# Both parts of v in one operand for both directions of an mLSTM, with the second sum in the bank of the scores

## The chip, the cores and the metric

The kernel runs on one core of a Trainium2 chip. Its engines are TensorE (PE in the profile, with PEld for the loads of its weights), VectorE (DVE), ScalarE (ACT), GpSimd (POOL) and SyncE (SP), whose queue issues most of the transfers. The time is what the device takes for one launch, in microseconds (us). Before the change three runs took 2744.58, 2746.43 and 2747.94 us; the median is 2746.43.

## The reference

One encoder layer is applied to two sequences, of 1024 and 2048 tokens, each with 16 meta tokens in front. One projection of the normalised input feeds two branches, a windowed attention over a grid and a bidirectional mLSTM; both are gated, projected, merged and put out through a last projection. What matters here is the chunkwise mLSTM, which runs once forwards and once on the flipped sequence:

```python
def _encoder_layer(h, ...):
    xn = _rmsnorm(h, g_pre)
    proj = xn @ w_in + b_in
    ya = (_neighbourhood_attention(...) * silu(na_z)) @ w_a
    yb = (_mlstm_branch(...) * silu(ml_z)) @ w_b
    y = (ga * ya + gb * yb) @ w_out
    return h + _rmsnorm(y, g_post)

def _mlstm_chunkwise(q, k, v, ig, lf):
    ...
    S = einsum('bhnjd,bhnsd->bhnjs', q, k) * exp(logD - m_t[..., None])
    e_inter = exp(inter - m_t)
    num = einsum('bhnjs,bhnsv->bhnjv', S, v) + e_inter[..., None] * einsum('bhnvk,bhnjk->bhnjv', Cs, q)
    den = sum(S, -1) + e_inter * einsum('bhnk,bhnjk->bhnj', ns, q)
    return num / maximum(abs(den), exp(-m_t))[..., None]
```

All data are 32-bit floats.

## The kernel before

**Products of split numbers.** Every 32-bit operand of a product is split into a high part, rounded to the format that TensorE multiplies at full pace, and a low part, the rest. `mm3` (L165) adds three products: high by high, high by low, low by high. The last one, low by low, is dropped.

**Two programs woven into one.** TensorE runs in the order in which the program is written; the order on the other engines is set by a scheduler that knows the dependences. `run` walks through two generators. `dense` yields after every few products of the projections (L170 to L172 with 512 columns, L607 to L609 with 256, L1592 to L1594) and says what they cost; `sparse` goes through the four steps mLSTM of the short sequence, attention of the short one, mLSTM of the long one, attention of the long one. Each time that `sparse` yields a cost, so much of `dense` is written before `sparse` goes on. One yield in the mLSTM has the cost 1.82 (`A_A`): between two of its steps stand 6 or 12 products of 512 columns, or as many columns in products of 256.

**The mLSTM.** The 96 chunks of 128 tokens (four heads, 8 chunks of the short and 16 of the long sequence) are taken two at a time, as 48 blocks. `ml_states` makes the states of a head; `ml_outputs` then goes through its blocks b with p = b - 1 behind it. In one turn of its loop are six yields. `scores(b)` makes the products of k and q (L1344, L1345) in the one bank `sc` of PSUM and copies a part with ScalarE (L1347); `scores_up(b)` adds the other part on VectorE (L1352) and multiplies by the decays of the two directions (L1357, L1358); `scores_lo(b)` makes the low parts (L1364). `back(p, j)` is the output of chunk j of the block before: the state's part with three products of 260 columns into a bank `tr` (L170 to L172), scaled by ScalarE into `num` (L1377, twice), and the part with v into a bank `sm`, added to `num` by VectorE (L1383, L1384). For direction 0 of that part the operand is `v2`, where the high part of v (130 columns: 128, a column of ones for `den`, and one of zeros) and the low part lie side by side, so that one product of 258 columns (L1380) and one of 130 (L1381) do for three; direction 1 takes `mm3` with three products of 130 columns. One bank has 512 columns; the two directions use 388. `decay`, `conv_*`, `load`, `kv` and `state` prepare the next block; `finish(p)` divides.

PSUM has eight banks: three `pj` for the projections, two `tr`, one `sc`, two `sm`. A bank is handed on only when its last reader is through.

**x, and where it is kept.** `build_half` makes the operand x of 512 tokens of the long sequence: rows of the mean squares by a product with ones (`rrows`, L329, copied by ScalarE at L330), then eight scalings on VectorE (L477), four roundings on ScalarE (L484) and four subtractions on VectorE (L485). For the short sequence it is L343 and L344. A half that is needed again later is stored in memory in 16 pieces of 256 KB, put in the queue `xput` by `xkeep`; `beside`, which is called after every yield of `dense`, issues one of them in every second call (L503), and `xparts` issues what is left before the next half is built (L334).

**The attention's start.** `na` loads for its first head q, k, v and the gate (`na_prep`, L847 to L862), then the position bias (`na_bias`, L835), all through the queue of SP.

Of the kernel before, what the change touches and what calls it, by code (L numbers as in the profile page):

```python
# [13 lines left out]
ALU = mybir.AluOpType  # L14
# [3 lines left out]
P = 128  # L18
# [41 lines left out]
def _row_types(R):  # L60

    out = []
    for t in range(R // 8):
        if t == 0:
            out.append((0, 0, 11))
        elif t == R // 8 - 1:
            out.append((2, R - 12, 12))
        else:
            out.append((1, 8 * t - 4, 15))
    return out  # L70
# [48 lines left out]
A_NA, A_D, A_A, A_G = 1.085, 1.63, 1.82, 1.3  # L119


class K:
# [376 lines left out]
    def beside(self):  # L499

        self.turn += 1
        if self.xput and self.turn % 2:
            self.nc.sync.dma_start(*self.xput.popleft())  # L503


# [262 lines left out]
    def na(self, s, rts):  # L768

        tc, nc, i = self.tc, self.nc, self.i  # L770
        rows = _row_types(SEQLEN[s] // 64)
        with tc.tile_pool(name=f"na{s}{rts[0]}", bufs=1, side="right", reuse_waits="tile") as np_:
            self.qB = [np_.tile([P, 4, P], F32R, name=f"qB{j}") for j in range(2)]
            self.kx = [np_.tile([P, 16, 64], F32R, name=f"kx{j}") for j in range(2)]
            self.gts = [np_.tile([P, 17, 48], F32, name=f"gt{j}") for j in range(2)]
            for q in self.qB:
                nc.gpsimd.dma_start(q[64:128], i["onehot"].rearrange("a (b c) -> a b c", b=4))
            for g in self.gts:
                nc.gpsimd.memset(g[:, 0, :], 0.0)
                nc.gpsimd.memset(g[:, 16, :], 0.0)  # L780
            heads = [(rt, pr, hh) for rt in rts for pr in range(4) for hh in range(2)]
            n = len(heads)
            prep = self.na_prep(np_, s, rows, heads, 0)
            for k in range(6):
                next(prep, None)
                for _ in range(2 if k else 17 - 11 * s):
                    yield A_NA
            self.na_bias(rows, heads, 0)
            cur, nxt = self.head, None
            units = [(j, cb) for j in range(n) for cb in range(4)]  # L790
            ready = {}
            n_ = len(units)
            for u in range(n_ + 4):
                if u >= 4:
                    self.na_copy(ready[u - 4])
                if u < n_:
                    j, cb = units[u]
                    if cb == 0:
                        cur = self.head
                        prep = self.na_prep(np_, s, rows, heads, j + 1) if j + 1 < n else iter(())  # L800
                        next(prep, None)
                    ready[u] = [cur, heads[j], cb, None, None, self.gts[j % 2], None]
                    self.na_scores(np_, ready[u], rows)
                    if j + 1 < n and cb == 0:
                        self.na_bias(rows, heads, j + 1)
                yield A_NA
                if u < n_:
                    self.na_exp(np_, ready[u])
                if 1 <= u <= n_:
                    self.na_scale(np_, ready[u - 1])  # L810
                if u >= 4:
                    self.na_add(ready.pop(u - 4), s)
                if u < n_ and cb:
                    next(prep, None)
                if u == n_ + 3:
                    break
                yield A_NA
                if 2 <= u <= n_ + 1:
                    self.na_turn(np_, ready[u - 2])
                    if u < n_ and cb >= 2:  # L820
                        next(prep, None)
                yield A_NA
                if 2 <= u <= n_ + 1:
                    self.na_low(ready[u - 2])
                if u >= 3:
                    self.na_out(ready[u - 3])
                yield A_NA
# [426 lines left out]
    def ml_outputs(self, mp, s, h, g, NB, sts, norms):  # L1254

        nc = self.nc
# [18 lines left out]
        def gates(b):  # L1275

            if b % 2:
                tzs[b // 2] = [mp.tile([P, 4, P], F32, name=n, tag="tz", bufs=2) for n in ("tog", "szg")]
                for x, d in zip(tzs[b // 2], (self.TO, self.SZ)):
                    nc.sync.dma_start(x, d[s][(b - 1) * BL:(b + 1) * BL, h * P:(h + 1) * P].rearrange("(c p) f -> p c f", p=P))  # L1280

        def conv_a(b):
            if b < NB:
                convs[b] = self.conv(mp, raws.pop(b), h, False, BL)
                next(convs[b])
# [15 lines left out]
        def kv(b):  # L1301
            if b < NB:
                kf = kfs.pop(b)
                kh = mp.tile([P, CB, P], F32R, name="kh", tag="kh", bufs=2)
                kl = mp.tile([P, CB, P], F32R, name="kl", tag="kl", bufs=2)
                nc.scalar.activation(f2(kh), kf, AF.Copy)
                nc.vector.tensor_tensor(f2(kl), kf, f2(kh).bitcast(F32), op=ALU.subtract)
                kss[b] = kh, kl
# [30 lines left out]
        def scores(b):  # L1339

            (kh, kl), (qh, _, q2) = kss.pop(b), qs[b]
            s0 = self.psum("sc", [P, CB, 2, P])
            for j in range(CB):
                nc.tensor.matmul(s0[:, j], kh[:, j], q2[:, j], start=True, stop=False)  # L1344
                nc.tensor.matmul(s0[:, j, 0], kl[:, j], qh[:, j], start=False, stop=True)  # L1345
            s1 = mp.tile([P, CB, P], F32, name="s1", bufs=1)
            nc.scalar.activation(s1, s0[:, :, 1], AF.Copy)  # L1347
            shs[b] = s0, s1

        def scores_up(b):  # L1350
            s0, s1 = shs[b]
            nc.vector.tensor_tensor(s1, s0[:, :, 0], s1, op=ALU.add)  # L1352
            sh = mp.tile([P, 2, CB, P], F32R, name="sh", tag="bh", bufs=2)
            sl = mp.tile([P, 2, CB, P], F32R, name="sl", tag="bl", bufs=2)
            for d in range(2):
                um = ums[b][d]
                nc.vector.tensor_tensor(um, um, s1, op=ALU.mult)  # L1357
                nc.scalar.activation(f2(sh[:, d]), f2(um), AF.Copy)  # L1358
            shs[b] = sh, sl
# [6 lines left out]
        def back(b, j):  # L1366
            sh, sl = shs[b]
            (vh, vl, v2), (qh, ql, _) = vs[b], qs[b]
            cch, ccl = cs[b]
            cc = 1 + b * CB + j  # L1370
            pi = self.psum("tr", [P, 512])
            self.mm3(pi[:, :260], qh[:, j, :], ql[:, j, :], cch[:, j], ccl[:, j])
            if j == 0:
                nums[b] = mp.tile([P, CB, 2, 130], F32, name="num", bufs=1)
            num = nums[b]
            for d in range(2):
                nc.scalar.activation(num[:, j, 1 - d], pi[:, 130 * d:130 * d + 130], AF.Copy, scale=g[d]["e"][:, cc, h:h + 1])  # L1377
            pa = self.psum("sm", [P, 512])
            self.mm3(pa[:, 0:130], sh[:, 1, j, :], sl[:, 1, j, :], vh[:, j, :], vl[:, j, :])
            nc.tensor.matmul(pa[:, 130:388], sh[:, 0, j, :], v2[:, j, 0:258], start=True, stop=False)  # L1380
            nc.tensor.matmul(pa[:, 130:260], sl[:, 0, j, :], vh[:, j, :], start=False, stop=True)  # L1381
            nj = num[:, j].rearrange("p d c -> p (d c)")
            nc.vector.tensor_tensor(nj, pa[:, :260], nj, op=ALU.add)  # L1383
            nc.vector.tensor_tensor(num[:, j, 1, 0:P], pa[:, 260:388], num[:, j, 1, 0:P], op=ALU.add)  # L1384

        def finish(b):
            num = nums.pop(b)
# [32 lines left out]
        for b in range(NB + 1):  # L1420
            p = b - 1
            if p >= 0:
                gates(p)
            if b < NB:
                scores(b)
                conv_a(b + 1)
            yield A_A
            if p >= 0:
                back(p, 0)
            if b < NB:  # L1430
                scores_up(b)
            yield A_A
            if b < NB:
                scores_lo(b)
            conv_b(b + 1)
            load(b + 2)
            decay(b + 1, 0)
            yield A_A
            if p >= 0:
                back(p, 1)  # L1440
            decay(b + 1, 1)
            conv_c(b + 1)
            yield A_A
            kv(b + 1)
            if p >= 0:
                finish(p)
            yield A_A
            state(b)
            yield A_A

# [361 lines left out]
```

## Time and profile before

| | |
|---|---|
| median of three runs | 2746.43 us |
| the profiled execution | 2745.8 us |
| its span in the trace | 2744.0 us |
| granted TensorE clock, mean | 0.999 |
| share of the span: PE, PEld, DVE, ACT, POOL | 99%, 89%, 66%, 49%, 1% |
| transfers | 661.08 MB, mean 241 GB/s |
| chain of waits that ended last, shares of the span | PE 94%, DMA 4%, DVE 1% |

Work before the first instruction and behind the last of the span takes 1.8 us (2745.8 - 2744.0). A row of a group gives line, engine, operation, tile written <- tiles read, shape, count | busy time in us, mean ns of one | idle time of the engine just before them and what ended it. A row of the order of time gives the start in us from the span's start, the duration, and then the same, with the idle time in brackets. Starts of a product and of its weights' load overlap with what runs before them, so the pace of TensorE is read from the distances of starts and not from durations.

### The profile page before, as it was taken

Reading aid. Unit: us, or ns where it says so; the run is one execution under the profiler, and the core shown is the slowest. Engines: PE = TensorE matmul, PEld = TensorE weight load, DVE = VectorE, ACT = ScalarE, POOL = GpSimd, SP = SyncE. Lnnn points to the kernel's source line nnn. Section 1 sums busy time; section 2 is a strip of 40 time slices with the busy share of each in tenths; the row PEclk is TensorE's granted clock in tenths of the full one; section 3 lists DMA queues with packets and bytes.
Section 4 is the critical chain, followed back from the end, with each engine's and each line's share of the span. In section 5 each row is a group of like instructions: output and inputs, shape, how many; then the busy total and the mean of one; then the engine's idle time right before and its main releaser. Section 6 shows DMA issues by size and latency. Waiting matters only on the chain.

```text
span 2744.0 us, 48160 instructions
## 1 busy us (share of the span) xinstructions
PE 2724.6 (99%) x16888; PEld 2429.5 (89%) x16888; DVE 1801.9 (66%) x5082; ACT 1343.7 (49%) x3236; POOL 16.1 (1%) x104
## 2 busy tenths in 40 slices
PE   9999999999999999999999999999999999999998
PEld 8998898999789988988988888888888989989898
DVE  5332688766556755467768667575668788897854
ACT  5122556445444454255566655564555655556421
POOL 0000000000000000000000000000000000000000
PEclk9999999999999999999999999999999999999999
DMA  9655768855875644686866689577559798999965
GB/s 368 201 183 196 254 212 318 273 165 199 312 222 159 193 143 135 179 314 218 275 233 233 234 293 307 180 240 233 181 192 308 231 337 255 319 293 281 322 238 204
DMA packets 375203, 661.08 MB, mean 241 GB/s; under 512 B 46800, under 2 KB 195744, under 8 KB 374960
## 3 DMA queue, kind: packets, MB, share of 16 engines
q1 hardware_dynamic: 373840, 655.31, 71.7%
q0 software_dynamic: 1120, 2.69, 0.5%
q8 instruction: 133, 2.18, 0.3%
q14 instruction: 110, 0.90, 0.1%
HBM read 455.64 MB, written 202.22 MB: 240 GB/s over the span
## 4 chain that ended last, share of the span: by engine, by line
PE 94%; DMA 4%; DVE 1%; ACT 0%; issue 0%; SPq 0%; DVEq 0%; ACTq 0%
PE pj L170 17%; PE pj L171 17%; PE pj L172 17%; PE pj L607 7%; PE pj L608 7%; PE pj L609 7%; PE pj L1592 3%; PE pj L1594 3%; PE pj L1593 3%; PE sm L946 3%; PE tr L931 3%; DMA wraw<-wu 1%; PE sm L172 1%; PE sm L171 1%; PE sm L170 1%; PE sc L899 1%
## 5 line engine op out<-in xcount | busy, mean ns | idle before, releaser
L170 PE MATMUL pj<-xh,whi 128*128 128x512 f32 (+1 forms) x1792 | 704.7, 393 | 0.7 <-ACT whi L264 0.6
L171 PE MATMUL pj<-xl,whi 128*128 128x512 f32 (+1 forms) x1792 | 688.7, 384 | 0.1
L172 PE MATMUL pj<-xh,wlo 128*128 128x512 f32 (+1 forms) x1792 | 687.9, 384 | 0.3 <-DVE wlo L265 0.3
L607 PE MATMUL pj<-whi,xh 128*128 128x256 f32 (+1 forms) x1536 | 439.6, 286 | 1.6 <-DMA whi<-wh 1.6
L608 PE MATMUL pj<-wlo,xh 128*128 128x256 f32 (+1 forms) x1536 | 433.2, 282 | 1.9 <-DMA wlo<-wl 1.9
L609 PE MATMUL pj<-whi,xl 128*128 128x256 f32 (+1 forms) x1536 | 433.0, 282 | 0.0
L172 PEld LDWEIGHTS pj<-xh,wlo 128*128 128x128 f32 x1792 | 337.0, 188 | 71.9 <-DVE wlo L265 0.5
L170 PEld LDWEIGHTS pj<-xh,whi 128*128 128x128 f32 x1792 | 337.0, 188 | 60.5 <-ACT whi L264 1.4
L171 PEld LDWEIGHTS pj<-xl,whi 128*128 128x128 f32 x1792 | 337.5, 188 | 57.3 <-issue 1.0
L607 PEld LDWEIGHTS pj<-whi,xh 128*128 128x128 f32 x1536 | 290.0, 189 | 2.5 <-DMA whi<-wh 1.9
L608 PEld LDWEIGHTS pj<-wlo,xh 128*128 128x128 f32 x1536 | 289.9, 189 | 2.6 <-DMA wlo<-wl 2.4
L609 PEld LDWEIGHTS pj<-whi,xl 128*128 128x128 f32 x1536 | 289.9, 189 | 0.0
L1592 PE MATMUL pj<-whi,mh 128*128 128x256 f32 x768 | 217.0, 283 | 0.7 <-DMA whi<-wh 0.7
L1594 PE MATMUL pj<-whi,mlo 128*128 128x256 f32 x768 | 216.7, 282 | 0.0
L1593 PE MATMUL pj<-wlo,mh 128*128 128x256 f32 x768 | 216.6, 282 | 0.0
L938 DVE TENSOR_TENSOR pts<-tr,pts 96x384 fp32r<-96x384 f32 (+2 forms) x192 | 119.1, 620 | 85.6 <-ACT pts L933 83.5
L933 ACT ACTIVATE pts<-tr 96x384 fp32r<-96x384 f32 (+2 forms) x192 | 103.8, 541 | 130.2 <-PE tr L931 129.4
L170 PE MATMUL pj<-yh,whi 128*128 128x512 f32 x384 | 155.1, 404 | 0.0
L171 PE MATMUL pj<-yl,whi 128*128 128x512 f32 x384 | 151.0, 393 | 0.8 <-DVE yl L1494 0.8
L172 PE MATMUL pj<-yh,wlo 128*128 128x512 f32 x384 | 151.2, 394 | 0.0
L1592 PEld LDWEIGHTS pj<-whi,mh 128*128 128x128 f32 x768 | 145.4, 189 | 1.9 <-DMA whi<-wh 0.9
L1593 PEld LDWEIGHTS pj<-wlo,mh 128*128 128x128 f32 x768 | 145.4, 189 | 1.0
(294 smaller groups left out, 4992.1 us busy)
## 6 DMA issues: line engine op xcount, KB each, us to landing
whi<-wh SPq DMA_DIRECT2D x192, 512.0 KB
wlo<-wl SPq DMA_DIRECT2D x192, 512.0 KB
wraw<-wu SPq DMA_DIRECT2D x64, 512.0 KB
wh<-whi SPq DMA_DIRECT2D x64, 512.0 KB
wl<-wlo SPq DMA_DIRECT2D x64, 512.0 KB
gt<-st SPq DMA_DIRECT2D x96, 256.0 KB
tg<-gt SPq DMA_DIRECT2D x96, 256.0 KB
xt<-xt SPq DMA_DIRECT2D x32, 512.0 KB
```

What stands on the lines that cost most here:

```text
L170: mm(out, ah, bh, start=start, stop=False)
L171: mm(out, ah, bl, start=False, stop=False)
L172: mm(out, al, bh, start=False, stop=stop)
L607: nc.tensor.matmul(o, xh, wh, start=k == 0, stop=False)
L608: nc.tensor.matmul(o, xh, wl, start=False, stop=False)
L609: nc.tensor.matmul(o, xl, wh, start=False, stop=k == KT - 1)
L931: nc.tensor.transpose(pt[:ks, ch, :], pr_[:, ch * ks:(ch + 1) * ks], self.ident)
L933: nc.scalar.activation(pts[:ks, :nb, 0, :], pt[:ks, :nb], AF.Copy)
L938: self.nc.vector.tensor_tensor(pts[:ks, :nb, 1, :], pt[:ks, :nb], pts[:ks, :nb, 0, :].bitcast(F32), op=ALU.subtract)
L1592: nc.tensor.matmul(o, mh[:, k, xs], wh, start=clear > 0 and k == 0, stop=False)
L1593: nc.tensor.matmul(o, mh[:, k, xs], wl, start=False, stop=False)
L1594: nc.tensor.matmul(o, ml[:, k, xs], wh, start=False, stop=clear < 2 and k == KT - 1)
```

## The change

There are four edits. In `back`, both directions now take `v2` with a product of 258 columns and one of 130; direction 0 sums in a bank `sm`, direction 1 in the bank `sc`; each sum is added to `num` by two instructions on VectorE, of 130 and 128 columns, where before one of 260 and one of 128 served both. In the loop of `ml_outputs` the two calls of `back` come one yield later, and `kv` and `finish` move around the yield behind them. `beside` issues a piece of the kept x in every fourth call in place of every second. In `na` the bias of the first head is loaded ahead of the rest.

```diff
@@ beside
-        if self.xput and self.turn % 2:
+        if self.xput and self.turn % 4 == 1:
             self.nc.sync.dma_start(*self.xput.popleft())
@@ na
             prep = self.na_prep(np_, s, rows, heads, 0)
+            self.na_bias(rows, heads, 0)
             for k in range(6):
...
-            self.na_bias(rows, heads, 0)
@@ back
-            pa = self.psum("sm", [P, 512])
-            self.mm3(pa[:, 0:130], sh[:, 1, j, :], sl[:, 1, j, :], vh[:, j, :], vl[:, j, :])
-            nc.tensor.matmul(pa[:, 130:388], sh[:, 0, j, :], v2[:, j, 0:258], start=True, stop=False)
-            nc.tensor.matmul(pa[:, 130:260], sl[:, 0, j, :], vh[:, j, :], start=False, stop=True)
-            nj = num[:, j].rearrange("p d c -> p (d c)")
-            nc.vector.tensor_tensor(nj, pa[:, :260], nj, op=ALU.add)
-            nc.vector.tensor_tensor(num[:, j, 1, 0:P], pa[:, 260:388], num[:, j, 1, 0:P], op=ALU.add)
+            for d in range(2):
+                pa = self.psum("sc" if d else "sm", [P, 512])
+                nc.tensor.matmul(pa[:, 0:258], sh[:, d, j, :], v2[:, j, 0:258], start=True, stop=False)
+                nc.tensor.matmul(pa[:, 0:130], sl[:, d, j, :], vh[:, j, :], start=False, stop=True)
+                for c in (0, 130):
+                    nj = num[:, j, 1 - d, 0:130 if not c else P]
+                    nc.vector.tensor_tensor(nj, pa[:, c:c + nj.shape[1]], nj, op=ALU.add)
@@ ml_outputs, the loop
             yield A_A
-            if p >= 0:
-                back(p, 0)
             if b < NB:
                 scores_up(b)
             yield A_A
+            if p >= 0:
+                back(p, 0)
             if b < NB:
                 scores_lo(b)
             conv_b(b + 1)
             load(b + 2)
             decay(b + 1, 0)
             yield A_A
-            if p >= 0:
-                back(p, 1)
             decay(b + 1, 1)
             conv_c(b + 1)
             yield A_A
+            if p >= 0:
+                back(p, 1)
             kv(b + 1)
+            yield A_A
             if p >= 0:
                 finish(p)
-            yield A_A
             state(b)
             yield A_A
```

## The prediction

> **What bounds the kernel now.** I read the page's busy times first, then the waits of TensorE, then the order of time around one call of `back`, and at last the stretch where VectorE is fullest.
>
> ```profile
> span 2744.0 us, 48160 instructions
> PE 2724.6 (99%) x16888; PEld 2429.5 (89%) x16888; DVE 1801.9 (66%) x5082; ACT 1343.7 (49%) x3236; POOL 16.1 (1%) x104
> ```
>
> TensorE is the bound: 19.4 us of the span (2744.0 - 2724.6) are without a product. So a product less is worth its slot, and a new wait of TensorE costs its full length. Waits are few and short; these are three of the largest:
>
> ```profile
> PE pj L608 <- DMA wlo<-wl: 1.9, 2, 1.0
> PE pj L607 <- DMA whi<-wh: 1.6, 1, 1.6
> PE sc L899 <- ACT kd L877: 0.9, 1, 0.9
> ```
>
> None lies in `back`. VectorE is busy for two thirds of the span on average, but not evenly; that decides below.
>
> **The product that goes.** The order of time around one call of `back`, weights' loads (PEld) and what follows:
>
> ```profile
> 1602.74 0.28 PE L170 MATMUL tr<-cch,q 128*128 128x260 f32 x1
> 1602.86 0.19 PEld L172 LDWEIGHTS tr<-cch,q 128*128 128x128 f32 x1
> 1602.98 0.19 PEld L170 LDWEIGHTS sm<-v,sh 128*128 128x128 f32 x1
> 1603.10 0.19 PEld L171 LDWEIGHTS sm<-v,sh 128*128 128x128 f32 x1
> 1603.21 0.19 PEld L172 LDWEIGHTS sm<-v,sl 128*128 128x128 f32 x1
> 1603.32 0.19 PEld L1380 LDWEIGHTS sm<-v,sh 128*128 128x128 f32 x1
> 1603.43 0.19 PEld L1381 LDWEIGHTS sm<-v,sl 128*128 128x128 f32 x1
> 1603.53 0.62 ACT L1377 ACTIVATE num<-tr,g_eT 128x130 f32<-128x130 f32 x2
> 1603.55 0.19 PEld L170 LDWEIGHTS pj<-xh,whi 128*128 128x128 f32 x1
> 1604.18 0.43 DVE L1383 TENSOR_TENSOR num<-sm,num 128x260 f32<-128x260 f32 x1 [1.22 <-ACT num L1377]
> 1604.64 0.29 DVE L1384 TENSOR_TENSOR num<-sm,num 128x128 f32<-128x128 f32 x1
> ```
>
> Loads follow each other at 0.12 us behind a product of 260 or 258 columns (1602.98 - 1602.86; 1603.55 - 1603.43) and at 0.11 behind one of 130 (1603.21 - 1603.10). So a narrow product takes nearly the slot of a wide one. Direction 1 had three slots of 0.11; it gets one of 0.12 and one of 0.11, 0.10 less. There are as many calls as rows of L1380:
>
> ```profile
> L1380 PE MATMUL sm<-v,sh 128*128 128x258 f32 x96 | 32.0, 333 | 0.0
> ```
>
> 96 x 0.10 = 9.6 us; with the slot read as 0.114 ((1603.55 - 1602.98) / 5) it is 10.9 less a little for the wider operand. I take -10.2. Bounds: if the slot were only the columns at the pace of 260 in 0.12, three of 130 cost 0.18, 258 + 130 columns the same, and nothing is gained; -10.9 at the other end. I stay near the rows' own distances.
>
> [...]
>
> **The four sums on VectorE.** For 260 + 128 columns in two instructions come 130 + 128 twice. Distances of back-to-back instructions and what else is needed, from the fullest stretch:
>
> ```profile
> 468.19 0.42 DVE L1298 TENSOR_TENSOR q<-cv,q 128x256 fp32r<-128x256 f32 x1
> 468.52 0.28 DVE L1384 TENSOR_TENSOR num<-sm,num 128x128 f32<-128x128 f32 x1
> 468.72 0.16 DVE L1391 SCALAR_TENSOR_TENSOR den<-num 128x4 f32<-128x4 f32 x1
> 468.79 0.69 DVE L1336 TENSOR_TENSOR ccl<-st,cch 128x520 fp32r<-128x520 f32 x1
> ...
> 469.89 2.73 DVE L477 SCALAR_TENSOR_TENSOR xt<-xt,gpre,rx 128x512 f32<-128x512 f32 x4
> 473.92 0.48 DVE L1108 SCALAR_TENSOR_TENSOR cv<-raw,cw,cv 128x256 f32<-128x256 f32 x1
> 474.32 0.76 DVE L1314 TENSOR_TENSOR um<-um,trim 128x256 f32<-128x256 f32 x2
> 474.99 1.22 DVE L485 TENSOR_TENSOR xl<-xt,xh 128x1024 fp32r<-128x1024 f32 x1
> ```
>
> A sum of 128 columns occupies 0.20 (468.72 - 468.52), one of 256 0.33 (468.52 - 468.19). The new four take 0.80, the old two 0.53: 96 x 0.27 = 26 us more on VectorE, which has 942 us free. In a usual block nothing of it reaches TensorE; if all of it did, it would cost the 26.
>
> **The new wait.** A sum in `sc` binds TensorE to VectorE. The second product of `back(p, 0)` must wait until L1352 has read the scores; that of `back(p, 1)` until the sums of `back(p, 0)` are done; the next scores until those of `back(p, 1)` are. Before, two banks `sm` gave a sum room until the call after next. Behind the waiting product stand, on TensorE, the projections, so nothing else fills the gap; their evacuations and weights come later by as much, and no end is met sooner.
>
> In a usual block there is room. From the start of `back` to the end of L1384 pass 2.2 us above (1604.64 + 0.29 - 1602.74), 0.3 more with four sums. The order of the changed program has 13 or more slots between two calls: 12 products of 512 at 0.23 (row of L171 to row of L172 below) and the call's own 0.8, 3.6 us.
>
> Moving `back` and `finish` by a yield is free: they issue no transfers, `num` and `v2` are next written three yields later, and ScalarE is 49% busy. If that cover is gone, a late `v2` or `num` stops TensorE as a late sum does, within the bounds below.
>
> The room ends where x is built. VectorE was busy for all of one such stretch:
>
> ```profile
> 469.90:486.70 16.80, 16.80 (x84) 14.04 (x83) 16.80 (x39) 12.36 (x28) 0.00 (x0) 1.00 1.04 369
> ```
>
> How it starts, on TensorE and ScalarE:
>
> ```profile
> 467.49 1.07 PE L329 MATMUL pj<-xr,ones 128*128 128x512 f32 x2
> 468.63 0.39 PE L171 MATMUL pj<-xl,whi 128*128 128x512 f32 x1
> 468.86 0.39 PE L172 MATMUL pj<-xh,wlo 128*128 128x512 f32 x1
> 468.84 0.59 ACT L330 ACTIVATE rx<-pj 128x512 f32<-128x512 f32 x1
> ```
>
> L330 ends 1.94 us after L329 starts; L329 holds TensorE for 0.9 (468.63 - 0.23 - 467.49). In the changed order of VectorE there stand, from then to the last sum of the same block's second call: six L477 (0.68 each), L1298, L1325 and two L1314 (0.33), L1336 (0.62), one L485 (1.14, its 1.22 less the overlap of the others), four sums: 4.1 + 1.3 + 0.6 + 1.1 + 0.8 = 7.9, done at 9.8. TensorE has 18 products of 512 (4.2), one call (0.8) and L329 until the next scores: 5.9. It waits 3.9. From there VectorE has until the last sum of the next block's first call three L485, two L477, four L1108 (0.40), six of 256 columns, one as long as L1336, ten of 128 (0.20) and small ones of 0.35 together: 3.4 + 1.4 + 1.6 + 2.0 + 0.6 + 2.0 + 0.4 = 11.4. TensorE has scores (0.5), 36 products (8.4), a call (0.8) and five slots (0.6): 10.3. It waits 1.1 more: 5.0 in this build. After it comes the last block of a head, without scores, and VectorE catches up.
>
> The build at the end of the short sequence's mLSTM has eight L477 and the sums, with a few small ones, ahead: 1.94 + 6.4 = 8.3 against 7.9 on TensorE (L329, 24 products, a call, five slots), 0.4. A third place, where L343 and L344 make x late in the long sequence, I take at 0.8, between these two and nearer to the smaller, since each of its pieces is short. All together +6.2. Below nothing is excluded: a bank that is asked for later than before frees nobody sooner. The other bound is the latest sum of now:
>
> ```profile
> 475.82 0.28 PE L170 MATMUL tr<-cch,q 128*128 128x260 f32 x1
> 479.54 0.28 PE L170 MATMUL tr<-cch,q 128*128 128x260 f32 x1
> 486.37 0.29 DVE L1384 TENSOR_TENSOR num<-sm,num 128x128 f32<-128x128 f32 x1
> ```
>
> It ended 10.8 us after its call, when the next call had been 3.7 after it: 7.1 of wait, if the changed kernel were as late.
>
> **The transfers.**
>
> ```profile
> 740.00:760.00 20.00, 19.11 (x84) 15.33 (x83) 7.21 (x12) 7.29 (x12) 0.00 (x0) 1.00 1.03 333
> 760.00:780.00 20.00, 16.49 (x85) 13.92 (x85) 7.38 (x21) 7.79 (x16) 0.00 (x0) 0.94 1.04 340
> 738.52 2.18 SPq L503 DMA_DIRECT2D xl<-xl  x3
> 750.07 1.11 SPq L835 DMA_DIRECT2D gt<-rpb  x2
> ```
>
> The waits for weights (1.9 + 1.6) lie in the second stretch, with the transfers' share full (1.04). Storing half as often moves pieces out of the burst and, for the first half of a group, into the flush of `xparts`: eleven in place of five in the changed order of SP. The bytes stay. I count 0, with -3.5 (the waits go) and +3.5 (doubled) as bounds. The bias ahead of q and k puts one issue of 0.55 (1.11 / 2) on SP before the loads on which L899 waited 0.9: between 0 and +0.55 in the two attentions each, +0.3 in all.
>
> **The sum.** -10.2 + 6.2 + 0.3 = -3.7 on the profiled execution's 2745.8: 2742.1 us. That execution is 0.6 under the median of 2746.43, so against the median it is -4.3, 0.16%.
>
> **The rivals.**
> - *VectorE keeps up.* The scheduler knows the new dependence and may put sums earlier than I counted; the changed order does set four sums side by side in most blocks. Against it: in two of the three places work of x stands ahead of the sums. Without any wait: 2745.8 - 10.2 + 0.3 = 2735.9.
> - *Slower: VectorE is late in every build.* Three of the builds with L477 lie beside mLSTM blocks of the short sequence; each costs the 7.1 of now's latest sum, from the first on, since ScalarE's roundings are late too and my sums leave out its queue. 2745.8 - 10.2 + 0.3 + 3 x 7.1 = 2757.2. For it: VectorE was full for 16.8 us on end. Against it: TensorE's wait itself lets VectorE catch up. It decides from 3.4 us per build on, where the gain is used up. [...]
> - *The change doesn't do what it says: nothing gained per slot.* Only columns count, and the waits stay: 2745.8 + 6.2 + 0.3 = 2752.3. The rows of 0.11 speak against it.
> - *The weights' waits change.* 2742.1 - 3.5 = 2738.6, or 2745.6.
>
> **How the numbers follow.** The forecast 46%, with its own range 2737 to 2746; VectorE keeps up 19%; late in every build 21%; nothing gained 5%; weights 9%, both ways. What a measurement can tell from no change is 0.2%, 5.5 us: faster is under 2740.9, slower over 2751.9. Faster: 0.17 of the forecast, 0.19, and 0.06 of the weights: 0.42. Slower: the 0.21, 0.03 of nothing gained and 0.01 of the forecast: 0.25. Same: 0.33. The range, 2734 to 2757, reaches from just under the second case to the third's figure.
>
> **What would show it.** Right: 96 products fewer, four loads between the state's products and the projections, spaced 0.11 to 0.12; new waits of TensorE in L1344 and in the product into `sc` on L1384, a few us, all near L477, L485 or L344; none in other blocks. Wrong: waits of that kind spread over the 48 blocks, or ten us in one build; slots of 0.17 or more for the rest; waits on weights of another size than 3.5.

## The result, and the profile after

| | before | after |
|---|---|---|
| median (12 runs each, run side by side) | 2745.84 us | 2753.86 us |
| lowest to highest | 2744.05 to 2751.46 | 2748.86 to 2758.06 |
| the profiled execution, its span | 2745.8, 2744.0 | 2755.1, 2753.4 |
| granted TensorE clock, mean | 0.999 | 0.995 |

The ratio is 1.0029, with a 95% interval of 1.0022 to 1.0037: the change makes the kernel 8 us slower. The forecast was 2742.1, 4 us faster; the range, 2734 to 2757, holds the time, but the sign is wrong.

The head of the page of the changed kernel:

```profile
span 2753.4 us, 48230 instructions
PE 2721.6 (99%) x16792; PEld 2422.7 (88%) x16792; DVE 1819.9 (66%) x5274; ACT 1342.9 (49%) x3236; POOL 16.0 (1%) x104
```

96 products fewer, as written. But the span without a product has grown from 19.4 to 31.8 us (2753.4 - 2721.6), by 12.4. The waits of TensorE say where (engine, tile and line that waited <- what ended it: us in all, times, longest):

```profile
PE sc L1344 <- DVE den L1391: 9.3, 4, 3.8
PE sc L899 <- ACT kd L877: 2.8, 1, 2.8
PE pj L329 <- ACT sh L1358: 2.0, 1, 2.0
...
PE sc L1380 <- DVE num L1384: 1.6, 1, 1.6
...
PE sc L1380 <- DVE s L1352: 1.0, 1, 1.0
```

9.3 + 1.6 + 1.0 = 11.9 us are waits for the bank `sc`, 2.0 are new at L329, L899 has gone from 0.9 to 2.8. The three waits for weights of before at L607 and L608, 3.5 us, are gone; one of 0.3 stands at L172.

That is not all. The stretches of the changed kernel in which the granted clock is below 1, and then the only such stretch of before; the start and the end of the program, where both have one, are left out. A row gives the stretch and its length, then the busy time (and count) of PE, PEld, DVE, ACT and POOL, then the granted clock, the share of the transfers' engines and GB/s:

```profile
474.00:482.00 8.00, 6.96 (x20) 5.69 (x21) 7.95 (x18) 3.75 (x10) 0.00 (x0) 0.57 1.06 360
690.00:698.00 8.00, 5.96 (x21) 4.29 (x21) 7.42 (x27) 2.54 (x7) 0.00 (x0) 0.79 0.32 98
762.00:770.00 8.00, 5.47 (x18) 4.49 (x19) 3.23 (x7) 4.21 (x8) 0.00 (x0) 0.79 1.02 350
1866.00:1874.00 8.00, 6.45 (x19) 5.22 (x20) 6.97 (x22) 3.86 (x10) 0.00 (x0) 0.57 0.11 38
```

```profile
776.00:782.00 6.00, 5.72 (x34) 5.72 (x35) 3.59 (x11) 3.34 (x7) 0.00 (x0) 0.72 1.05 345
```

A mean of 0.57 over 8 us takes 8 x 0.43 = 3.4 us, one of 0.79 takes 1.7, that of before (6 x 0.28) also 1.7: always once or twice the same amount. The clock is halved (0.50 granted from 476 to 480 us) for 3.4 us or for 6.8, behind the longest waits or from their last half microsecond on. The changed kernel has six such stretches of 3.4 us and before one, which makes at most 5 x 1.7 = 8.5 us. So the span's +9.4 is +12.4 idle, up to +8.5 slow clock, and what is left, -11.5, is the products that went. The 8.5 is a little too much: two of the stretches begin 0.6 and 0.5 us before their wait ends, and a slot at half the clock is 0.43 us in place of 0.23 (last section), not twice as long. With both, an estimate, the clock takes 5 x 3.4 x (1 - 0.23 / 0.43) - 1.1 x 0.47 = 7.4, and -10.4 is left for the products.

How the longest wait comes about, VectorE and TensorE in the order of time:

```profile
470.86 0.39 PE L172 MATMUL pj<-xh,wlo 128*128 128x512 f32 x1
470.92 0.42 DVE L1298 TENSOR_TENSOR q<-cv,q 128x256 fp32r<-128x256 f32 x1
...
471.26 0.29 DVE L1384 TENSOR_TENSOR num<-sm,num 128x130 f32<-128x130 f32 x1
471.46 0.28 DVE L1384 TENSOR_TENSOR num<-sc,num 128x130 f32<-128x130 f32 x1
...
473.28 1.22 DVE L485 TENSOR_TENSOR xl<-xt,xh 128x1024 fp32r<-128x1024 f32 x1
...
474.61 0.28 DVE L1384 TENSOR_TENSOR num<-sc,num 128x128 f32<-128x128 f32 x1
...
475.04 0.55 PE L1344 MATMUL sc<-q,kh 128*128 128x256 f32 x1 [3.79 <-DVE den L1391]
```

The scores' other input, `q`, is ready at 471.3. The bank is not: between its two sums VectorE works at the next block's operands and at x for 2.9 us, and TensorE has 3.79 us of nothing.

And the slots of a call, by the loads of the weights:

```profile
1608.73 0.19 PEld L1380 LDWEIGHTS sm<-v,sh 128*128 128x128 f32 x1
...
1608.86 0.19 PEld L1381 LDWEIGHTS sm<-v,sl 128*128 128x128 f32 x1
...
1608.98 0.19 PEld L1380 LDWEIGHTS sc<-v,sh 128*128 128x128 f32 x1
...
1609.09 0.19 PEld L1381 LDWEIGHTS sc<-v,sl 128*128 128x128 f32 x1
...
1609.21 0.19 PEld L170 LDWEIGHTS pj<-xh,whi 128*128 128x128 f32 x1
```

Four slots in 0.48 us, where five took 0.57. The gain was there; it was lost elsewhere.

### The profile page after: what moved, and what is told of

It reads as the page before. It is cut to its first block, busy times and chain, and to the rows that moved or that the text cites. A ratio compares the mean times of both kernels' runs of the same rounds, so it can differ in the third digit from the quotient of the medians.

```text
span 2753.4 us, 48230 instructions
## 1 busy us (share of the span) xinstructions
PE 2721.6 (99%) x16792; PEld 2422.7 (88%) x16792; DVE 1819.9 (66%) x5274; ACT 1342.9 (49%) x3236; POOL 16.0 (1%) x104
## 4 chain that ended last, share of the span: by engine, by line
PE 92%; DMA 3%; DVE 3%; ACT 1%; issue 1%; SPq 0%; DVEq 0%; ACTq 0%
PE pj L170 16%; PE pj L172 16%; PE pj L171 16%; PE pj L607 6%; PE pj L609 6%; PE pj L608 6%; PE pj L1593 3%; PE pj L1592 3%; PE pj L1594 3%; PE sm L946 3%; PE tr L931 3%; PE sc L899 1%; PE sc L900 1%; PE sm L899 1%; PE sm L900 1%
## 5 line engine op out<-in xcount | busy, mean ns | idle before, releaser
L172 PE MATMUL pj<-xh,wlo 128*128 128x512 f32 (+1 forms) x1792 | 691.1, 386 | 0.6 <-DVE wlo L265 0.3
L607 PE MATMUL pj<-whi,xh 128*128 128x256 f32 (+1 forms) x1536 | 439.4, 286 | 0.0
L608 PE MATMUL pj<-wlo,xh 128*128 128x256 f32 (+1 forms) x1536 | 432.6, 282 | 0.0
L172 PEld LDWEIGHTS pj<-xh,wlo 128*128 128x128 f32 x1792 | 338.6, 189 | 73.2 <-DMA wlo<-wl 0.7
L607 PEld LDWEIGHTS pj<-whi,xh 128*128 128x128 f32 x1536 | 289.5, 188 | 0.6
L608 PEld LDWEIGHTS pj<-wlo,xh 128*128 128x128 f32 x1536 | 289.4, 188 | 0.2
L172 PE MATMUL pj<-yh,wlo 128*128 128x512 f32 x384 | 151.9, 396 | 0.0
```

Of the source, the lines that this page charges most:

```text
L172: mm(out, al, bh, start=False, stop=stop)
L607: nc.tensor.matmul(o, xh, wh, start=k == 0, stop=False)
L608: nc.tensor.matmul(o, xh, wl, start=False, stop=False)
```

## The experiments

Ten kernels, in the order in which they ran. Each was timed in five rounds beside the kernel before.

| kernel | median, us | ratio to before | 95% interval |
|---|---|---|---|
| `both_in_sm` | 2751.87 | 1.0018 | 1.0010 to 1.0027 |
| `old_transfers` | 2755.88 | 1.0030 | 1.0019 to 1.0042 |
| `one_product_less` | 2731.62 | 0.9940 | 0.9928 to 0.9953 |
| `filled_waits` | 2751.75 | 1.0023 | 1.0014 to 1.0032 |
| `one_bank` | 2731.27 | 0.9942 | 0.9929 to 0.9954 |
| `move_only` | 2748.67 | 1.0009 | 1.0000 to 1.0018 |
| `four_sums` | 2741.72 | 0.9984 | 0.9975 to 0.9992 |
| `old_order` | 2769.90 | 1.0081 | 1.0068 to 1.0094 |
| `transfers_only` | 2743.70 | 0.9991 | 0.9982 to 0.9999 |
| `one_bank_transfers` | 2731.47 | 0.9955 | 0.9942 to 0.9969 |

**`both_in_sm`: is it the bank of the scores?**

```diff
-                pa = self.psum("sc" if d else "sm", [P, 512])
+                pa = self.psum("sm", [P, 512])
```

> The changed kernel with one word changed: direction 1 sums in a bank `sm` like direction 0, so that `sc` holds the scores alone. Theory A (the bank of the scores, and the clock behind it): the changed kernel's 9.3 us of waits at L1344 and the 1.0 at L1380 for L1352 go, and with them four of its six stretches of 3.4 us at half the clock (1.7 each, 6.8); in `sm` a sum has until the next call, 3.6 us or more, which costs at most 3 us. 2753.9 - 10.3 - 6.8 + (0 to 3) = 2736.8 to 2739.8, ratio to before 0.997 to 0.998. Rival B (the move and the four sums make VectorE late, whatever the bank): the waits come back at the products into `sm` in the same places, ratio 1.002 to 1.003.

Theory A fell. TensorE waits in this kernel for the sums' own banks instead:

```profile
PE sm L1380 <- DVE num L1384: 7.9, 3, 6.3
PE sm L1380 <- DVE mv L1461: 2.6, 1, 2.6
```

7.9 + 2.6 = 10.5 us stand against 11.9, and the longest wait has grown to 6.3. Sharing with the scores is not the point: whichever bank it is, VectorE's sums come too late for it. Two explanations were left. Either the move and the two more sums make VectorE late, or it was late all along and the old kernel could afford it.

**`old_transfers`: the two edits of the transfers undone in the changed kernel.**

```diff
-        if self.xput and self.turn % 4 == 1:
+        if self.xput and self.turn % 2:
...
-            self.na_bias(rows, heads, 0)
             for k in range(6):
...
+            self.na_bias(rows, heads, 0)
```

> The changed kernel with the transfers as before: a piece of the kept x in every second call, the bias behind the other loads. Theory A: the wait of 2.8 us at L899 shrinks to 0.9 and its stretch at half the clock goes (1.7), while the weights' waits of 3.5 us and their stretch (1.7) come back: -3.6 + 5.2 = +1.6, ratio 1.003 to 1.004; the waits near x stay. Rival C (the transfers' order is what makes the changed kernel slow): the time goes back by most of 8 us, ratio below 1.001.

The ratio is as expected, and rival C is out: with the old transfers the changed kernel is as slow. The reason given was wrong, though. The wait at L899 stays (2.4 us), and the waits for weights at 770 us do not come back; one of 2.9 appears at another place, at 2409 us:

```profile
PE pj L1592 <- DMA whi<-wh: 3.4, 2, 2.9
PE sc L899 <- ACT kd L877: 2.4, 1, 2.4
```

**`one_product_less`: the first term by itself.** The kernel before, without the low part of the scores by the high part of v for direction 0.

```diff
-            nc.tensor.matmul(pa[:, 130:388], sh[:, 0, j, :], v2[:, j, 0:258], start=True, stop=False)
-            nc.tensor.matmul(pa[:, 130:260], sl[:, 0, j, :], vh[:, j, :], start=False, stop=True)
+            nc.tensor.matmul(pa[:, 130:388], sh[:, 0, j, :], v2[:, j, 0:258], start=True, stop=True)
```

> The kernel before without the low product of direction 0 (L1381): low part of the scores by high part of v is left out for one direction, 96 products of 130 columns fewer, nothing else. It measures the first term by itself. Slots as the rows show: -10.2, at most -11, ratio 0.9960 to 0.9963. By columns alone (0.055 us each): -5.3, ratio 0.9981.

Its page:

```profile
span 2727.0 us, 47966 instructions
PE 2712.2 (99%) x16792; PEld 2418.1 (89%) x16792; DVE 1798.2 (66%) x5082; ACT 1340.9 (49%) x3236; POOL 16.7 (1%) x104
```

The medians differ by 13.7 us, the spans by 17.0. Of these, 4.6 are idle time (19.4 - 14.8), because the waits for weights do not happen here, and 1.7 the slow stretch behind them. What is left, 10.7, belongs to 96 products: 0.11 us each. The account is that of one profiled execution of each kernel, and this one, at 2728.8, was the fastest of its five; but the time without a product and the slow stretch are taken out, and the busy time of TensorE says the same (2724.6 - 2712.2 - 1.7). The slot is right and the count of columns is out (5.3; with 130 columns at the pace of 512 in 0.23 us it would be 5.6, an estimate).

**`filled_waits`: what does the slow clock cost?** Products that nobody reads stand ahead of the scores of three blocks of the changed kernel.

```diff
             (kh, kl), (qh, _, q2) = kss.pop(b), qs[b]
+            fill = {(0, 1, 3): 30, (1, 3, 5): 13, (1, 3, 7): 24}.get((s, h, b), 0)
+            if fill:
+                pf = self.psum("tr", [P, 512])
+                for i in range(fill):
+                    nc.tensor.matmul(pf[:, 0:256], kh[:, 0], q2[:, 0], start=True, stop=True)
             s0 = self.psum("sc", [P, CB, 2, P])
```

> The changed kernel with products that nobody reads (256 columns, 0.12 us each, into a bank `tr`) ahead of the scores of the three blocks where TensorE waited longest: 30 for 3.8 us, 13 for 1.7, 24 for 3.1. The waits last as long as before, but TensorE works through them. Theory A (each such wait costs its length and then stretches of 3.4 us at half the clock): the four stretches behind the first and the third wait go, 4 x 1.7 = 6.8 less, ratio 1.0004. Rival D (the slow clock costs nothing, since VectorE is late there anyhow and TensorE would wait instead): the time stays, ratio 1.0029, with the saved 6.8 us as new waits.

The stretches behind the two longest waits are gone; the granted clock stays at 1.00:

```profile
470.00:484.00 14.00, 13.85 (x80) 11.88 (x79) 13.28 (x31) 9.39 (x21) 0.00 (x0) 1.00 1.04 362
1860.00:1876.00 16.00, 14.44 (x81) 12.21 (x81) 14.73 (x51) 10.31 (x22) 0.00 (x0) 1.00 0.43 141
```

The stretch behind L899 is gone as well: that wait of 2.8 us came as two here, 0.8 and 1.5. With TensorE busy in the place of its wait, the clock of that time is 1.00 and not 0.57, so in these runs it is TensorE's idleness that halves its clock. But only a part of the time comes back. The line numbers of this kernel are five higher; its product into `sc` waits here, at 716 us (1.6) and 488 us (1.9), where the changed kernel did not. The second 1.6 of the first row, at 1846 us, was there before:

```profile
PE sc L1385 <- DVE num L1389: 3.3, 2, 1.6
...
PE sc L1385 <- DVE mv L1466: 1.9, 1, 1.9
```

The median is 2.1 us below the changed kernel's, the profiled span 3.8, and the intervals of the two ratios overlap, so the timing alone does not decide between A (6.8) and D (0). The traces show both at work: the clock is regained, and VectorE, which needs the same time beside a slow TensorE (1.22 us for an L485 of the changed kernel, within the stretch behind 474 us as outside it), takes a part of it back as waits. How much the clock costs by itself stays open between 2 and 7 us.

**`one_bank`: the saved product with the old kernel's room.** This tells the two explanations apart. 258 columns twice do not fit into a bank of 512 (`self.psum("sm", [P, 512])`), so the column of zeros and the low part of one of v's 128 columns are left out: 256 twice.

```diff
-                v2 = mp.tile([P, CB, 260], F32R, name="v2", bufs=1)
-                vh, vl = v2[:, :, 0:130], v2[:, :, 130:260]
-                nc.scalar.activation(vh, va, AF.Copy)
-                nc.vector.tensor_tensor(vl, va, vh.bitcast(F32), op=ALU.subtract)
+                v2 = mp.tile([P, CB, 256], F32R, name="v2", bufs=1)
+                vh, vl = v2[:, :, 0:129], v2[:, :, 129:256]
+                nc.scalar.activation(vh, va[:, :, 0:129], AF.Copy)
+                nc.vector.tensor_tensor(vl, va[:, :, 0:127], v2[:, :, 0:127].bitcast(F32), op=ALU.subtract)
...
             pa = self.psum("sm", [P, 512])
-            self.mm3(pa[:, 0:130], ...)
...
+            for d in range(2):
+                c = 256 * (1 - d)
+                nc.tensor.matmul(pa[:, c:c + 256], sh[:, d, j, :], v2[:, j], start=True, stop=False)
+                nc.tensor.matmul(pa[:, c:c + 130], sl[:, d, j, :], v2[:, j, 0:130], start=False, stop=True)
+            pv = pa.rearrange("p (d c) -> p d c", d=2)
+            for a, n in ((0, 129), (129, 127)):
+                nj = num[:, j, :, 0:n]
+                nc.vector.tensor_tensor(nj, pv[:, :, a:a + n], nj, op=ALU.add)
```

> The kernel before, with its loop order and transfers, but both directions take both parts of v (256 columns and 130) and share one bank `sm` per call, 512 columns in all, with two sums on VectorE. For that the low part of one of v's 128 columns and the column of zeros are left out. Theory A2 (room: VectorE was always late near x, and the changed kernel, with two banks per call, takes away the time until the call after next that hid it): no new wait, so only the gain of the first term is left, -10.8 as measured, with the weights' waits anywhere between kept and gone (-5): ratio 0.994 to 0.9965, faster than both kernels. Rival F (a product of 256 columns with its own weights costs more than its slot): ratio 0.998 or above.

Faster than both kernels, by 14.9 us against before. VectorE is late here too. Two calls of `back` during the build of x, the three calls of that time by their tile (first and last start), the sums, and the stretch as a whole:

```profile
474.07 0.28 PE L170 MATMUL tr<-cch,q 128*128 128x260 f32 x1
...
477.69 0.29 PE L170 MATMUL tr<-cch,q 128*128 128x260 f32 x1
```

```profile
L170 PE MATMUL tr<-cch,q x3: 277/277/286, 474.1 to 486.9; 128*128 128x260 f32 x3
```

```profile
482.01 0.75 DVE L1386 TENSOR_TENSOR num<-sm,num 128x258 f32<-128x258 f32 x2
...
485.58 0.41 DVE L1386 TENSOR_TENSOR num<-sm,num 128x254 f32<-128x254 f32 x1
```

```profile
470.00:490.00 20.00, 20.00 (x100) 16.73 (x99) 19.42 (x54) 13.15 (x31) 0.10 (x1) 1.00 1.04 371
```

The first sums of both calls begin at 482.01, 7.9 us after the first call and 4.3 after the second; a last sum starts at 485.58. TensorE is busy for all of the 20 us at full clock: the second call has a bank of its own, and the third, which needs the first one's again, comes at 486.9, when that last sum has ended at 485.99. That is 8.3 us behind its call (485.99 - 477.69); in the kernel before, the latest sum ended 10.8 behind, also without a wait. Theory A2 holds. The late VectorE was in the old kernel too, and what the change took away is the room that hid it. In the changed kernel only the sums in `sc` have lost it: `sm` still has two banks for one sum per call, and no wait for a sum in `sm` is among its rows. One difference besides the banks is left: this kernel adds with two instructions per call and the changed one with four. `four_sums` below shows that these are free where there is room, but not what they add where there is none.

**`move_only` and `old_order`: the move by itself, and the changed kernel without it.** In `move_only` the loop of the changed kernel stands in the kernel before, in `old_order` the loop of before in the changed kernel (the lines of the diff of `ml_outputs` above).

> The kernel before with the changed kernel's loop order and nothing else: products, sums, banks and transfers stay. Theory A2: a sum still has until the call after next, no wait near x; the 2.0 us of wait at L329 that the later `finish` made may come, with a stretch at half the clock: 2745.3 + (0 to 3.7), ratio 1.0000 to 1.0013. Rival B (the move makes VectorE's sums too late): waits of 5 us or more at the products into `sm` and `sc`, ratio 1.003 or above.

> The changed kernel with the loop order of before. Theory A2: the same two banks per call, so waits near x of the same size or larger, since the product into `sc` now follows the scores by 2.4 us and must wait for L1352: 10 to 20 us of waits, 2752 to 2760, ratio 1.002 to 1.005. Rival B (the move is the cause): waits near x gone, ratio 0.997 to 0.999.

The move alone gives +2.5 us, at the edge of what can be told from nothing (the interval begins at 1.0000). Its trace says more. Its waits:

```profile
PE sc L1344 <- DVE q L1298: 2.2, 1, 2.2
PE sc L899 <- ACT kd L877: 2.2, 1, 2.2
PE pj L329 <- DVE mv L1461: 2.1, 1, 2.1
```

None is for a sum, as A2 wants. Each is an operand that VectorE or ScalarE made a little later, and each brings its slow stretch; of before's waits for weights only 0.9 is left at L608, and that hides a part of the cost in the median. The wait at L899 is not the move's alone: `transfers_only` below has it too, without the move. Without the move the new products are far worse, more than the 10 to 20 us expected:

```profile
PE sc L1380 <- DVE num L1384: 17.6, 5, 6.6
PE sc L1380 <- DVE s L1352: 10.0, 8, 2.9
```

27.6 us in 13 waits, 8 of which are for L1352. So rival B is out both ways: the move protects the change from the larger part of its own waits.

**`four_sums`: more instructions on VectorE alone.**

```diff
-            nc.vector.tensor_tensor(nj, pa[:, :260], nj, op=ALU.add)
-            nc.vector.tensor_tensor(num[:, j, 1, 0:P], pa[:, 260:388], num[:, j, 1, 0:P], op=ALU.add)
+            for c in (0, 130):
+                nc.vector.tensor_tensor(nj[:, c:c + 130], pa[:, c:c + 130], nj[:, c:c + 130], op=ALU.add)
+            for c in (0, 64):
+                nc.vector.tensor_tensor(num[:, j, 1, c:c + 64], pa[:, 260 + c:324 + c], num[:, j, 1, c:c + 64], op=ALU.add)
```

> The kernel before with the same sums cut into four instructions (130, 130, 64, 64 columns) on VectorE and nothing else. Prediction's term: 0, hidden, since a sum has until the call after next: ratio 1.000. Rival E (two more instructions per call are what makes VectorE late): waits of several us at L1380 or L170 near x, ratio 1.002 or above.

No wait for a sum, so rival E is out. That it is faster, by 4.4 us, with more work and no less, was not expected. Its page and its wait for weights:

```profile
span 2738.9 us, 48363 instructions
PE 2722.0 (99%) x16888; PEld 2428.6 (89%) x16888; DVE 1810.4 (66%) x5274; ACT 1343.5 (49%) x3236; POOL 16.6 (1%) x104
```

```profile
PE pj L608 <- DMA wlo<-wl: 0.9, 1, 0.9
```

16.9 us without a product in place of 19.4, and no slow stretch near 777: 2.5 + 1.7 = 4.2. The old kernel's three waits for weights between 770 and 777 us, with the stretch behind them, look like a chance meeting of transfers. None of the ten kernels has all three waits or that stretch, whatever its edit; five keep one wait of 0.9 at L608. So up to 4 us of every gain against before may be owed to it. This goes by one trace of each kernel and is not shown for before's other executions.

**`transfers_only` and `one_bank_transfers`: the two edits of the transfers on the kernel before and on the best one.**

> The kernel before with the two edits of the transfers alone: a piece of the kept x in every fourth call, the bias of the attention's first head ahead of its other loads. The prediction took +0.3 with 3.5 us either way for the waits for weights: ratio 0.9988 to 1.0014. If the transfers are a part of the loss: a longer wait at L899 (2 us or more) with a stretch at half the clock, ratio 1.0015 or above. If they help: the waits for weights of 3.5 us and their stretch (1.7) gone, ratio 0.998 to 0.9985.

> The kernel with both directions in one bank (order of before, the low part of one of v's 128 columns left out) and the two edits of the transfers. If the transfers act for themselves, the ratio is that of the one bank, 0.9942, times what the transfers alone give; if only the place in time of the bursts matters, the two differ from that product by more than 0.001.

Alone they give -1.7 us: the waits for weights are gone, and one at L899 of 2.2 us, with its slow stretch, takes their place.

On the kernel with one bank L899 waits 0.8, with the old transfers as with the new, and the medians are 0.2 us apart. It is 2.8 and 2.4 in the changed kernel with the new and the old transfers, and 0.8 in `both_in_sm` with the new. So these edits do not decide whether it is long; that it hangs on where the attention's start falls is likely, but not shown. The product of the two ratios, 0.9933, is further than 0.001 from 0.9955, but the intervals are too wide (0.9942 to 0.9969 for the one, 0.9929 to 0.9954 for the other factor) to call that shown.

## Why the prediction was wrong, step by step

- *A product less is worth its slot.* Right. -10.2 was forecast; 10.7 were measured by themselves, and the account of the changed kernel leaves 10.4 to 11.5. The slots came out as drawn, 0.11 to 0.13 apart.
- *The four sums are hidden.* Right where the banks give room, by `four_sums`. Their price was too high: VectorE's busy time grew by 18.0 us in the changed kernel (1819.9 - 1801.9) and not by 26.
- *The new wait.* The mechanism and its first place were right: 3.9 us forecast at the scores of the first build, 3.79 measured. The size was not: 6.2 in all against 11.9. The further 1.1 in that build and the 0.4 in the build at the end of the short sequence did not come; two waits, 1.0 at 1428 us and 0.8 at 1489, lie at no build of x, where none was forecast. The term that was mis-sized most is the third place, the builds of L343 and L344 late in the long sequence, taken at 0.8 "since each of its pieces is short". The pieces run in a row. In the changed kernel:

```profile
1862.26 3.40 DVE L344 SCALAR_TENSOR_TENSOR xl<-xt,gpre,xh 128x512 fp32r<-128x512 f32 x5 [1.99 <-ACT xh L343]
...
1867.12 0.28 DVE L1384 TENSOR_TENSOR num<-sc,num 128x128 f32<-128x128 f32 x1
...
1867.55 0.55 PE L1344 MATMUL sc<-q,kh 128*128 128x256 f32 x1 [3.06 <-DVE den L1391]
```

  Five pieces hold VectorE for 3.40 us on end, then `q` and the sums follow, and TensorE waits 3.06. The same happened at 1835 us (1.67). At 1846 us (1.63) the pieces are through, but VectorE has had no gap since 1831.6 and is only now at the end of the block before (L1402, L1455 and L1459, 1843.24 to 1846.4), with which the sums have to share. I take it for the wake of the build. Together 6.4 in place of 0.8.
- *"A new wait of TensorE costs its full length."* This step failed most: a wait of 2 us or more cost its length and then, in 20 of 23 cases (last section), a stretch at half the clock, for which the sum had no term. The row for it was in the profile of before, 0.72 from 776 to 782 us behind the waits for weights; the prediction itself shows 0.94 from 760 to 780, and I read the waits there without the column of the clock. It is 7.4 to 8.5 us in the account of the span, though not all of it can be had back: `filled_waits` was only 2 to 4 us faster.
- *"Moving `back` and `finish` by a yield is free."* Failed, by the trace of `move_only`: three new waits of 2.1 to 2.2 us, one of which other edits bring too, each with a slow stretch. The median, +2.5, does not show it by itself. I looked for transfers and for who writes `num` next, but not for what else stands in VectorE's queue at that moment. At 690 us the later `finish` and the norm behind it stand ahead of the operand of `rrows`; its second half (L323) ends at 692.13, and L329 starts at 692.22 after 2.04 us of waiting:

```profile
691.66 0.47 DVE L323 TENSOR_SCALAR xr<-ident,nwy 128x128 f32<-128x128 f32 x2
...
692.22 1.44 PE L329 MATMUL pj<-xr,ones 128*128 128x512 f32 x2 [2.04 <-ACT sh L1358]
```

- *The transfers at 0, between -3.5 and +3.5.* Alone they are -1.7, inside. In the changed kernel the forecast +0.3 at L899 was 1.9, with a slow stretch; `move_only` has most of that wait without any edit of a transfer, and `transfers_only` has as much without the move.
- *The rivals.* "VectorE is late in every build" gave 2757.2 and "nothing gained per slot" 2752.3; both lie near the 2755.1 of the profiled execution, and both by luck. The first counted three builds at 7.1 us. Of these the one at 423 us has no wait at all, the one at 467 has 3.8 us of wait and up to 3.4 of slow clock, and the one at 694 has 2.0 and 1.7, but for an operand and not for a sum. The rest lies in the long sequence, of which this rival says nothing. "Nothing gained" is out by the slots, "VectorE keeps up" by the waits.
- *The range.* It holds the time only because it was drawn out to the figure of the slower rival; the forecast's own range ended at 2746.

Not tried: a kernel with two banks per call and the whole low part of v in which VectorE does its sums ahead of the work on x; and the changed banks with two sums per call in place of four. So what the two more instructions add to the waits is not known by itself.

## What to carry to other kernels

In these runs a bank of PSUM was handed on at the pace of its slowest reader: `sc` at 475.04 us, when VectorE's last sum had ended at 474.89. So count, for each bank, the calls that may pass until it is asked for again, and compare them with the latest sum in the trace: a change that spreads a call's sums over two banks, or over a bank that another product needs, takes that room away (10.5 to 27.6 us of waits in `both_in_sm`, the changed kernel and `old_order`), even if it hardly touches the busy shares (VectorE had 66% before and after). Where one engine is busy for 99% of the span, price a new wait of it by the granted clock behind the waits that are already there (0.72 from 776 to 782 us here). And before a gain of a few us is put down to an edit, look for waits in the old trace that any shift in time makes go away; here they may be worth 4 us of 15.

## What was not expected of the hardware

**The clock fell behind single waits of 2 us.** In the twelve traces of this study TensorE had some 120 waits between 0.3 and 1.9 us between the first and the last 12 us that stood by themselves, and behind none of them the granted clock fell. Of the fifteen between 2.0 and 2.9 us, twelve were followed by one stretch of 3.4 us at half the clock and three by none; of the eight from 3.06 us on, all by one or two. The same wait of 3.79 us gave two stretches in the changed kernel and one in `old_transfers`:

```profile
472.00:480.00 8.00, 4.21 (x15) 3.54 (x15) 8.00 (x20) 4.43 (x10) 0.00 (x0) 0.79 0.95 340
```

So in these traces a stretch has a fixed length, and whether a wait gets one depends on when it falls. The starts of the stretches of one trace lie whole multiples of 3.413 us apart: in the changed kernel the granted clock goes from 1.00 to 0.50 at 474.39, 692.85, 764.53 and 1867.03 us, 64, 21 and 323 such steps apart. With each trace cut into steps of this length, the idle time of TensorE within a step tells the cases apart: all 21 steps with 1.82 us or more of it were followed by a stretch, and none with 1.65 or less, out of 9564 steps in the twelve traces. Within a stretch about half a microsecond was enough for a second one: the five stretches with 0.51 us of idle time or more had a second behind them, the other 21, with 0.38 or less, had none. The wait of 3.79 us reaches 0.64 us into its stretch in the changed kernel and 0.38 in `old_transfers`. The wait of 2.04 us at L329 lies within one step of the changed kernel; in `old_transfers` it is cut in two, 1.23 and 0.81:

```profile
689.44:692.85 3.41, 1.37 (x7) 0.68 (x5) 3.41 (x16) 1.30 (x4) 0.00 (x0) 1.00 0.26 77
692.85:696.26 3.41, 3.41 (x10) 2.31 (x9) 2.83 (x10) 0.60 (x1) 0.00 (x0) 0.50 0.45 136
```

```profile
687.07:690.48 3.41, 2.18 (x12) 1.52 (x10) 2.97 (x12) 1.66 (x6) 0.00 (x0) 1.00 0.22 80
690.48:693.90 3.42, 2.61 (x11) 1.89 (x12) 3.19 (x16) 0.87 (x2) 0.00 (x0) 1.00 0.34 92
```

Waits that lie close added up: in the kernel before, 1.65 and 0.89 us within 2.9 us (773.35 to 776.28) gave one. They put 1.82 us of idle time into the 3.41 us ahead of 777.48, where the clock falls to 0.50.

**At half the clock the slot only nearly doubled.** Products of 512 columns followed each other in 0.43 us in the stretch at 694 us in the changed kernel, where 0.23 is usual:

```profile
693.89 0.63 PE L171 MATMUL pj<-xl,whi 128*128 128x512 f32 x1
...
694.32 0.63 PE L172 MATMUL pj<-xh,wlo 128*128 128x512 f32 x1
```
